# The low half of every weight block made by an adding DMA, in a two-layer decoder trunk on one core

## The chip, the cores and the metric

The kernel runs on one core of one Trainium2 chip. The metric is the device time of one execution in microseconds (us); lower is better. Before the change it is 1383.34 us, the median of three runs from 1379.25 to 1384.71 us.

The engines are named as in the profile: PE is TensorE's matrix multiply and PEld its weight load, DVE is VectorE, ACT is ScalarE, POOL is GpSimd, SP is SyncE. A "q" behind a name (SPq, POOLq) is that engine's sequencer, which waits and issues DMAs. L377 is line 377 of the kernel before. In the changed kernel the lines from 378 on are numbered one higher (L1191 of before is L1192 there), and the pair that is exchanged stands on L376 to L378.

## What is computed

The reference is a decoder trunk of two layers on a sequence of 512 tokens with a width of 1024, in float32. Cut to what matters:

```python
for l in range(2):
    hn = rms_norm(h, attn_norm[l])
    proj = hn @ w_in[l]                          # 1024 x 2592
    y_a = rwkv7_mixer(proj[..., :896], ...)      # delta-rule state, 4 heads of 64
    y_b = retention_mixer(proj[..., 896:1920], positions)
    y_c = mla_mixer(proj[..., 1920:], positions, ...)   # 8 heads, w_q_up and w_kv_up
    h = h + concat(y_a, y_b, y_c) @ w_out[l]     # 1024 x 1024
    gu = rms_norm(h, ffn_norm[l]) @ w_gate_up[l] # 1024 x 5632
    h = h + (silu(gu[..., :2816]) * gu[..., 2816:]) @ w_down[l]   # 2816 x 1024
return rms_norm(h, final_norm)
```

The large products are made with more than one pass of a reduced float32 format, "fp32r" in the profile. A factor x is written as a rounded part hi and a remainder lo, and a product w x is summed up from hi(w) hi(x), hi(w) lo(x) and lo(w) hi(x).

## The kernel before, in words

**Layout.** Activations are kept transposed, with features on the 128 partitions and the 512 tokens along a row. A product is a chain of 128 x 128 weight tiles, each multiplied into 128 x 512 activations, summed in a bank of PSUM.

**The weight stream.** All large weights lie in one long array in the order of use, cut into 204 blocks, most of them 128 partitions x 1024 floats (512 KB). For each block `load_next` (from L362) issues a DMA on SP into a raw tile `wr`, a rounding copy on ACT into `wh` (the hi part), and on DVE the subtraction `wr - wh` into `wl` (the lo part). For four blocks, 20, 30, 105 and 139, the subtraction is on POOL. Each of the three kinds of tile has three buffers. `wnext` (L380) keeps up to three converted blocks ready: whenever the program takes one, it queues the conversion of the next that is not yet ready. So the conversion of block n+2 is written down when block n is taken, and it must wait until PE has done with block n-1, whose buffers it takes over.

**The products.** `gemm` (L385) goes through the 128-row tiles of a block and issues three matmuls for each: `wh` with the high activations, `wh` with the low ones, `wl` with the high ones. PE runs in the order of the program, so `wl` is needed at the third matmul of a block. A full block is 24 matmuls. The blocks of the last part of the down projection have 768 columns and 18 matmuls.

**Stages.** In each layer come first the input projection with the three mixers (34 blocks), then the output projection, then the gate and up projections and the down projection, in three groups of 8, 8 and 6 blocks of 128 features. Two gate/up blocks make one block of hidden features: DVE scales both by the norm (L1188, L1190), ACT applies SiLU (L1189), POOL multiplies them (L1191), and `split` (L286 on ACT, L287 on DVE) makes their hi and lo parts. Before the gate and up projections POOL adds up squares for the norm (L316).

**What sets the order.** Each engine runs its own queue in order. The tile framework's scheduler places most instructions. Matmuls are pinned in program order. In the mixers several generators take turns in a small driver, with delays from the table `T`, and a table `EN` says which engine takes which small operation. The change touches neither table.

Of the kernel before, what the change touches and what calls it, by code (L numbers as in the profile page):

```python
# [11 lines left out]
F32 = mybir.dt.float32  # L12
# [3 lines left out]
AF = mybir.ActivationFunctionType  # L16
ALU = mybir.AluOpType
# [25 lines left out]
POOL_LO = (20, 30, 105, 139)  # L43
# [135 lines left out]
def tile_trunk(ctx: ExitStack, tc: tile.TileContext, a: dict, out: bass.AP, dbg=None):  # L179
    nc = tc.nc  # L180
    act, dve, pool, sp = nc.scalar, nc.vector, nc.gpsimd, nc.sync
# [20 lines left out]
    def nm(s):  # L202
        uid[0] += 1
        return f"{s}_{uid[0]}"
# [156 lines left out]
    def load_next(parts=1):  # L361
        if stream["next"] < len(shapes):  # L362
            i, j = shapes[stream["next"]]
            stream["next"] += 1
            t = wp.tile([P, i * j], F32, tag="wr", name=nm("wr"), bufs=NW)
            src = a["wts"][stream["off"] : stream["off"] + P * i * j].rearrange("(p n) -> p n", p=P)
            stream["off"] += P * i * j
            hi = wp.tile([P, i * j], F32R, tag="wh", name=nm("wh"))
            lo = wp.tile([P, i * j], F32R, tag="wl", name=nm("wl"))
            on = stream["next"] - 1  # L370
            for part in range(parts):
                z = slice(part * i * j // parts, (part + 1) * i * j // parts)
                stream["dma"] = sp.dma_start(t[:, z], src[:, z])
                if parts > 1:
                    tc.keep_in_program_order(stream["dma"])
                act.copy(hi[:, z], t[:, z])  # L376
                (pool if on in POOL_LO else dve).tensor_tensor(lo[:, z], t[:, z], hi[:, z].bitcast(F32), ALU.subtract)  # L377
            stream["ready"].append(tuple(z.rearrange("p (i j) -> p i j", i=i) for z in (hi, lo)))  # L378

    def wnext():  # L380
        while len(stream["ready"]) < 3 and stream["next"] < len(shapes):
            load_next()
        return stream["ready"].pop(0)
# [515 lines left out]
    def dense():  # L899
# [3 lines left out]
        for k in range(KT):  # L903
            if k < 2:
                tc.keep_in_program_order(sp.dma_start(h[0][:, k, :], a["xT"][:, k, :]))
                load_next(2) if k == 0 else None
            elif k % 2 == 0:
                tc.keep_in_program_order(sp.dma_start(h[k // 2], a["xT"][:, k : k + 2, :]))
                load_next(2) if k == 4 else None
            xg.append(pair(ua))  # L910
            act.activation(xg[k][0], hk(k), AF.Identity, scale=col("attn_norm", 0, k))
            dve.scalar_tensor_tensor(xg[k][1], hk(k), col("attn_norm", 0, k), xg[k][0].bitcast(F32), ALU.mult, ALU.subtract)
# [342 lines left out]
```

## Time and profile before

| | value |
|---|---|
| median of three runs | 1383.34 us (1379.25 to 1384.71) |
| the profiled execution's own time | 1382.67 us |
| its span, first to last instruction | 1380.9 us |
| mean granted TensorE clock | 0.982 |
| busy share of the span | PE 95%, DVE 58%, ACT 41%, POOL 17% |
| DMA | 130.84 MB, 95 GB/s on average |

The page of a profile lists busy time by engine, the span in 40 slices, the DMA queues, and the chain of work that ended last: beginning at the last instruction, each step goes back to what released it. A group's row reads: line, engine, operation, what it writes and reads, shape and count, then total busy time and the mean of one in ns, then the idle time of its engine just before, and what ended that. A row of the timeline starts with the start and the duration in us. A row of a view by windows gives the window, its length, and then for each engine the busy time with the number of instructions, the granted clock, the mean share of time that the 16 DMA engines were busy, and GB/s.

### The profile page before, as it was taken

The numbers are of one execution on the slowest core, as the hardware profiler recorded it, in microseconds if no ns is written. First come the engines' busy times: TensorE is split into PE (matmuls) and PEld (weight loads), VectorE is DVE, ScalarE is ACT, GpSimd is POOL, SyncE is SP. The second block draws the span as 40 slices with busy tenths as digits, with TensorE's granted clock in tenths as the row PEclk, the third lists the DMA queues.
The fourth block names the chain that finished last, engine by engine and source line by source line (L and its number), as shares of the span: only waits on it lengthen the run. The fifth ranks groups of instructions, "written<-read, shape, count | busy, mean of one in ns | idle before, by whom it ended". The sixth has DMA issues, their size and how long they took to land.

```text
span 1380.9 us, 16829 instructions
## 1 busy us (share of the span) xinstructions
PE 1313.5 (95%) x6478; PEld 1055.3 (76%) x6478; DVE 796.2 (58%) x1183; ACT 569.7 (41%) x944; POOL 238.7 (17%) x181
## 2 busy tenths in 40 slices
PE   7989988899999999999999898889999999999996
PEld 5778766578888888888877776756888888888884
DVE  7787856747544445344757696476564534543543
ACT  7844445826322232122575335367342212321333
POOL 1160321213110011001314401112131101100111
PEclk9999999999999999999999899999999999999998
DMA  6434421212222232322532424021233223333221
GB/s 235 125 99 140 96 76 32 77 61 92 97 102 92 92 107 92 101 97 73 174 97 81 111 85 85 31 85 54 76 107 105 94 92 95 104 93 105 89 80 61
DMA packets 65577, 130.84 MB, mean 95 GB/s; under 512 B 29044, under 2 KB 31764, under 8 KB 65496
## 3 DMA queue, kind: packets, MB, share of 16 engines
q1 hardware_dynamic: 64120, 128.14, 30.2%
q8 instruction: 51, 0.84, 0.3%
q10 hardware_dynamic: 1232, 1.09, 0.2%
q0 software_dynamic: 144, 0.52, 0.1%
q14 instruction: 30, 0.25, 0.1%
HBM read 117.40 MB, written 9.18 MB: 92 GB/s over the span
## 4 chain that ended last, share of the span: by engine, by line
PE 80%; DVE 10%; ACT 5%; issue 3%; POOL 1%; DMA 1%; SPq 0%; DVEq 0%; ACTq 0%; POOLq 0%
PE pd L232 72%; PE pm L232 7%; PE pm L239 1%; DVE wl L377 1%; DVE nmx L865 1%; DVE Sb L750 1%; ACT u L867 1%; ACT wh L376 1%; DVE u L608 1%; DMA wr<-in_wts_dram 0%; DVE r L296 0%; ACT L327 0%; ACT u L882 0%; DMA u<-in_xT_dram 0%; DVE u L609 0%
## 5 line engine op out<-in xcount | busy, mean ns | idle before, releaser
L232 PE MATMUL pd<-u,wh 128*128 128x512 f32 x3048 | 959.9, 396 | 7.6 <-ACT wh L376 6.4
L232 PEld LDWEIGHTS pd<-u,wh 128*128 128x128 f32 x3048 | 570.0, 189 | 135.3 <-issue 8.0
L232 PE MATMUL pd<-u,wl 128*128 128x512 f32 x1524 | 597.7, 392 | 0.0
L376 ACT CAST wh<-wr 128x1024 fp32r<-128x1024 f32 (+3 forms) x206 | 208.2, 1013 | 531.9 <-PE pd L232 353.9
L232 PEld LDWEIGHTS pd<-u,wl 128*128 128x128 f32 x1524 | 288.5, 189 | 61.0 <-DVE wl L377 0.2
L377 DVE TENSOR_TENSOR wl<-wr,wh 128x1024 fp32r<-128x1024 f32 (+3 forms) x202 | 283.3, 1404 | 59.8 <-ACT wh L376 57.0
L1191 POOL TENSOR_TENSOR r<-r,r 128x512 f32<-128x512 f32 x44 | 63.7, 1447 | 576.2 <-ACT wh L376 484.6
L1190 DVE TENSOR_TENSOR r<-pd,rB 128x512 f32<-128x512 f32 x44 | 30.4, 691 | 135.4 <-PE pd L232 135.4
L1197 DVE TENSOR_TENSOR u<-u,pd 128x512 f32<-128x512 f32 x48 | 33.0, 687 | 125.9 <-PE pd L232 125.9
L232 PE MATMUL pm<-u,u 32*32 32x32 f32 (+4 forms) x728 | 77.2, 287 | 24.9 <-DVE Sb L750 16.2
L232 PEld LDWEIGHTS pm<-u,u 32*32 32x32 f32 (+3 forms) x728 | 55.1, 162 | 48.6 <-DVE Sb L750 21.5
L316 POOL TENSOR_TENSOR acc<-acc,r 128x512 f32<-128x512 f32 x37 | 55.2, 1491 | 192.5 <-ACT r L315 192.1
L1188 DVE TENSOR_TENSOR r<-pd,rB 128x512 f32<-128x512 f32 x44 | 30.4, 691 | 67.7 <-PE pd L232 67.5
L286 ACT CAST u<-r 128x512 fp32r<-128x512 f32 x52 | 32.4, 623 | 78.5 <-POOL r L1191 63.5
L232 PE MATMUL pd<-u,u 96*128 96x512 f32 (+3 forms) x128 | 45.2, 459 | 2.7 <-ACT u L867 1.6
L287 DVE TENSOR_TENSOR u<-r,u 128x512 fp32r<-128x512 f32 x52 | 35.9, 689 | 18.9 <-ACT u L286 18.9
L239 PE MATMUL pm<-ident,u 128*128 128x128 f32 x188 | 33.5, 283 | 5.5 <-ACT r L773 2.0
L870 POOL TENSOR_SCALAR u<-u,rs 128x384 f32<-128x384 f32 x16 | 20.6, 1285 | 98.8 <-DVE rs L869 67.6
L865 DVE TENSOR_REDUCE nmx<-pd 128x1 f32<-128x256 f32 (+3 forms) x64 | 30.0, 481 | 11.7 <-PE pd L232 11.2
L239 PEld LDWEIGHTS pm<-ident,u 128*128 128x128 f32 x188 | 23.7, 145 | 13.1 <-ACT r L773 3.3
L321 DVE SCALAR_TENSOR_TENSOR u<-u,PC,u 128x512 fp32r<-128x512 f32 x24 | 32.0, 1342 | 2.6 <-ACT u L320 2.5
L867 ACT ACTIVATE u<-pd,nmx 128x512 f32<-128x512 f32 (+2 forms) x48 | 26.0, 546 | 11.9 <-DVE nmx L865 7.8
(243 smaller groups left out, 1142.9 us busy)
## 6 DMA issues: line engine op xcount, KB each, us to landing
wr<-in_wts_dram SPq DMA_DIRECT2D x174, 512.0 KB, 3.5
wr<-in_wts_dram SPq DMA_DIRECT2D x22, 384.0 KB, 3.1
u<-in_xT_dram SPq DMA_DIRECT2D x7, 512.0 KB, 6.7
tb<-tab_d SPq DMA_DIRECT2D x8, 256.0 KB, 4.9
r<-r SPq DMA_DIRECT2D x32, 64.0 KB, 2.0
h_d<-u SPq DMA_DIRECT2D x4, 512.0 KB, 2.6
u<-h_d SPq DMA_DIRECT2D x4, 512.0 KB, 3.6
wr<-in_wts_dram SPq DMA_DIRECT2D x4, 432.0 KB, 3.1
```

The costliest lines, as they stand in the source:

```text
L232: tc.keep_in_program_order(nc.tensor.matmul(o, lhsT, rhs, start=start, stop=stop, skip_group_check=True))
L239: tc.keep_in_program_order(nc.tensor.transpose(o, x, idn))
L286: act.copy(hi, src)
L287: E("e273").tensor_tensor(lo, src, hi.bitcast(F32), ALU.subtract)
L316: E("e302").tensor_tensor(acc, acc, q, ALU.add)
L321: dve.scalar_tensor_tensor(lo, t, g, hi.bitcast(F32), ALU.mult, ALU.subtract)
L376: act.copy(hi[:, z], t[:, z])
L377: (pool if on in POOL_LO else dve).tensor_tensor(lo[:, z], t[:, z], hi[:, z].bitcast(F32), ALU.subtract)
L865: dve.tensor_reduce(nmx, ps[:, 0:w], AX.X, ALU.max, negate=True)
L867: act.activation(pp[ib], ps[:, 0:w], AF.Exp, bias=nmx, accum_out=ssum)
L1191: E("e1171").tensor_tensor(t, t, u, ALU.mult)
L1197: dve.tensor_tensor(hk(m), hk(m), ps, ALU.add)
```

## The change

For every block, ACT now writes two tiles: first minus the raw weights into `wl` (an activation with scale -1, whose output is rounded to fp32r), then the rounded copy into `wh` as before. After the first of the two, a DMA issued on POOL's queue reads the same raw weights once more from HBM and adds them onto `wl`. The subtraction on DVE, or for four blocks on POOL, is gone, and the table `POOL_LO` is no longer used.

```diff
@@ -373,8 +373,9 @@
                 stream["dma"] = sp.dma_start(t[:, z], src[:, z])
                 if parts > 1:
                     tc.keep_in_program_order(stream["dma"])
+                act.activation(lo[:, z], t[:, z], AF.Identity, scale=-1.0)
+                pool.dma_start(lo[:, z], src[:, z], accum_op=ALU.add)
                 act.copy(hi[:, z], t[:, z])
-                (pool if on in POOL_LO else dve).tensor_tensor(lo[:, z], t[:, z], hi[:, z].bitcast(F32), ALU.subtract)
             stream["ready"].append(tuple(z.rearrange("p (i j) -> p i j", i=i) for z in (hi, lo)))
```

Two places show how the queues change. In these rows a number behind a tile's name only tells one buffer's use from another, and the brackets name the engines or DMA queues (DMAHW those of SP and ACT, DMASW that of POOL) whose semaphores the instruction waits for. The first place is POOL's queue at the first hidden features of layer 0. Before, it holds the sums of squares and the products alone:

```order
L316 TENSOR_TENSOR acc_2893<-acc_2893,r_661_3014 128x512 [waits Activation_49,Pool_49]
L1191 TENSOR_TENSOR r_679_3123<-r_679_3123,r_680_3124 128x512 [waits DVE_49,Activation_49]
L1191 TENSOR_TENSOR r_686_3163<-r_686_3163,r_687_3164 128x512 [waits DMAHW4_49,DVE_49,Activation_49]
L1191 TENSOR_TENSOR r_697_3234<-r_697_3234,r_698_3235 128x512 [waits DVE_49,Activation_49]
L1191 TENSOR_TENSOR r_708_3305<-r_708_3305,r_709_3306 128x512 [waits DVE_49,Activation_49]
```

The same place in the changed kernel:

```order
L316 TENSOR_TENSOR acc_2929<-acc_2929,r_658_3032 128x512 [waits Activation_49,Pool_49]
L316 TENSOR_TENSOR acc_2929<-acc_2929,r_661_3052 128x512 [waits Activation_49,Pool_49]
L377 DMA wl_3060<-in_wts_dram 128x1024 [waits DMASW4_49,Activation_49]
L377 DMA wl_3089<-in_wts_dram 128x1024 [waits DMASW5_49,Activation_49]
L377 DMA wl_3125<-in_wts_dram 128x1024 [waits DMASW6_49,Activation_49]
L377 DMA wl_3176<-in_wts_dram 128x1024 [waits DMASW7_49,Activation_49]
L1192 TENSOR_TENSOR r_679_3164<-r_679_3164,r_680_3165 128x512 [waits DVE_49,Activation_49]
L1192 TENSOR_TENSOR r_686_3205<-r_686_3205,r_687_3206 128x512 [waits DMAHW4_49,DVE_49,Activation_49]
L377 DMA wl_3217<-in_wts_dram 128x1024 [waits DMASW0_49,Activation_49]
L377 DMA wl_3249<-in_wts_dram 128x1024 [waits DMASW1_49,Activation_49]
L1192 TENSOR_TENSOR r_697_3278<-r_697_3278,r_698_3279 128x512 [waits DVE_49,Activation_49]
```

Between two products POOL now issues two adding DMAs. The first of each pair stands behind a product that waits for DVE and ACT.

The second place is ACT's queue at the start of the kernel, where the first two blocks are converted in halves. Before:

```order
L312 ACTIVATE acc_162<-u_72 128x512
L376 CAST wh_104<-wr_103 128x512 [waits DMAHW2_49]
L376 CAST wh_104<-wr_103 128x512 [waits DMAHW3_49]
L911 ACTIVATE u_116<-u_72,PC 128x512 [waits DMAHW4_49]
L911 ACTIVATE u_120<-u_73,PC 128x512 [waits DMAHW0_49]
```

In the changed kernel:

```order
L312 ACTIVATE acc_167<-u_72 128x512
L376 ACTIVATE wl_105<-wr_103 128x512 [waits DMAHW2_49]
L378 CAST wh_104<-wr_103 128x512
L376 ACTIVATE wl_105<-wr_103 128x512 [waits DMAHW3_49]
L378 CAST wh_104<-wr_103 128x512
L912 ACTIVATE u_118<-u_72,PC 128x512 [waits DMAHW4_49]
L912 ACTIVATE u_122<-u_73,PC 128x512 [waits DMAHW0_49]
```

Each half now passes through ACT twice, the negated copy first. The scaling of the inputs (L911, now L912) stands behind both.

## Prediction

> **What bounds the kernel now.** I read the page's busy times first, then a table by windows to separate the stages, then the chain of waits in the two mixers, then the timeline of single blocks.
>
> ```profile
> span 1380.9 us, 16829 instructions
> PE 1313.5 (95%) x6478; PEld 1055.3 (76%) x6478; DVE 796.2 (58%) x1183; ACT 569.7 (41%) x944; POOL 238.7 (17%) x181
> ```
>
> ```profile
> core 0: us, PE busy (x) PEld busy (x) DVE busy (x) ACT busy (x) POOL busy (x), PEclk, DMA share, GB/s
> 0.00:30.00 30.00, 23.09 (x77) 16.43 (x78) 22.45 (x34) 21.54 (x34) 6.67 (x12) 1.00 0.69 237
> 30.00:296.00 266.00, 242.60 (x1438) 190.56 (x1436) 194.09 (x384) 148.21 (x298) 62.22 (x48) 0.96 0.32 91
> 343.00:684.00 341.00, 340.64 (x1502) 281.45 (x1500) 162.42 (x162) 101.26 (x123) 39.93 (x27) 1.00 0.31 101
> 704.00:966.00 262.00, 238.89 (x1412) 183.48 (x1411) 183.44 (x370) 141.56 (x291) 60.69 (x48) 0.97 0.27 78
> 1016.00:1365.00 349.00, 348.64 (x1536) 287.72 (x1535) 158.39 (x155) 104.86 (x128) 40.76 (x29) 1.00 0.29 91
> ```
>
> In the two feed-forward stages (341 and 349 us) PE is idle for 0.4 us each: nothing done for DVE gains time there. In the two mixers (266 and 262 us) PE is idle 23 us each and DVE is busy for about 70% of the time, so a freed DVE can help there. The chain of waits inside these two windows says how much:
>
> ```profile
> by line: PE pd L232 42.5%; PE pm L232 16.6%; issue 4.4%; PE pm L239 4.0%; DVE wl L377 2.3%; DVE nmx L865 1.6%; DVE Sb L750 1.6%; ACT u L867 1.2%; DVE u L608 1.1%; POOL r L776 1.1%; DVE r L330 1.0%; DVE r L329 1.0%; DVE r L296 1.0%; DVE u L6
> by line: PE pd L232 31.5%; PE pm L232 17.6%; issue 7.5%; DVE nmx L865 3.3%; DVE wl L377 2.6%; PE pm L239 2.1%; ACT wh L376 1.8%; ACT u L867 1.8%; DVE u L608 1.6%; ACT L327 1.5%; DVE Sb L750 1.4%; DVE r L296 1.3%; ACT u L882 1.2%; DVE u L609
> ```
>
> The first row is the mixer of layer 0, the second that of layer 1. The subtraction L377 holds 2.3% of 266 us and 2.6% of 262 us of the chain: 6.1 + 6.8 = 12.9 us.
>
> **What the change moves.** Per full block these are the durations now:
>
> ```profile
> L376 ACT CAST wh<-wr 128x1024 fp32r<-128x1024 f32 x174 | 182.6, 1051 | 485.3 <-PE pd L232 327.9 <-issue 149.8 <-PE pm L232 7.2
> L377 DVE TENSOR_TENSOR wl<-wr,wh 128x1024 fp32r<-128x1024 f32 x170 | 253.6, 1492 | 57.7 <-ACT wh L376 55.1 <-DMA wr<-in_wts_dram 2.6
> L561 POOL DMA_DIRECT2D vf_d<-u x1: 749/749/749, 48.2 to 48.2; - x1
> vf_d<-u POOLq DMA_DIRECT2D x1, 512.0 KB, 4.0
> wr<-in_wts_dram SPq DMA_DIRECT2D x174, 512.0 KB, 3.5
> q1 hardware_dynamic: 64120, 128.14, 30.2%
> ```
>
> DVE loses its 1.49 us per block. ACT gains about another 1.05 us (the same shape as the cast). POOL gains 0.75 us of issuing, by the one DMA of 512 KB that it issues now, which lands 4.0 us after its issue. That DMA copies; an adding one stands nowhere in this trace. It must read the weights and the tile, then write. Queue q1's row gives the price of one pass: 30.2% of 1380.9 us for 128.14 MB, or 1.71 us for 0.524 MB on all 16 engines. So from issue to landing I bound it below by 4.0 us (adding is free) and above by 4.0 + 3 x 1.71 = 9.1 us (two more passes one behind the other, and a raw load in between). I take one more pass, 5.7 us, since the second read is the part that surely comes on top.
>
> [...]
>
> **Feed-forward: a longer latency under a long cover.** One steady block, and then a narrow one of the last down projection:
>
> ```profile
> 370.25 1.05 ACT L376 CAST wh<-wr 128x1024 fp32r<-128x1024 f32 x1 [3.86 <-issue]
> 371.27 1.28 POOL L1191 TENSOR_TENSOR r<-r,r 128x512 f32<-128x512 f32 x1 [9.60 <-DVE r L1190]
> 371.33 2.30 DVE L377 TENSOR_TENSOR wl<-wr,wh 128x1024 fp32r<-128x1024 f32 x1 [0.21 <-ACT wh L376]
> 375.69 1.05 ACT L376 CAST wh<-wr 128x1024 fp32r<-128x1024 f32 x1 [2.48 <-PE pd L232]
> 381.56 0.39 PE L232 MATMUL pd<-u,wl 128*128 128x512 f32 x1
> ```
>
> ```profile
> 1336.84 0.83 ACT L376 CAST wh<-wr 128x768 fp32r<-128x768 f32 x1 [1.36 <-PE pd L232]
> 1345.50 0.39 PE L232 MATMUL pd<-u,wl 128*128 128x512 f32 x1
> ```
>
> ACT converts the block at 370.25 as soon as PE has released its buffers, and PE first uses its low half at 381.56, two blocks of 5.44 us (370.25 to 375.69) and a little later. Now the low half is ready at 373.63. With the change ACT is done with it at 371.30, but POOL's order puts the product at 371.27 ahead of every second DMA, and it ends at 372.55. From there 381.56 leaves 9.0 us for a DMA of 5.7: 3.3 us to spare. The narrow block leaves 1345.50 - 1336.84 - 0.83 = 7.8 us for a DMA of three quarters of the bytes, 4.0 + 0.75 x 1.71 = 5.3. So in these stages I cost the edit at **0**. The cover is the two blocks ahead; without it, each us above 9.0 is paid every second block.
>
> The engines' room is thinner: per block one raw load of 1.71 us and two passes of 3.42 us make 5.13 of 5.44 us. The window 0 to 30 us moved 237 GB/s at a share of 0.69, or 1.53 us per pass, by which it is 4.6 of 5.44. Both fit, barely.
>
> **The start.**
>
> ```profile
> 5.74 0.60 ACT L376 CAST wh<-wr 128x512 fp32r<-128x512 f32 x1
> 7.41 0.63 PE L232 MATMUL pd<-u,wl 128*128 128x512 f32 x1
> 16.93 0.39 PE L232 MATMUL pd<-u,wl 128*128 128x512 f32 x1
> ```
>
> The first low half is wanted at 7.41, the second block's at 16.93. ACT ends the negated half at 5.74 + 0.60 = 6.34; with 5.7 us it lands at 12.0, 4.6 us late. The next matmuls then come faster than they did, because they waited for the input, but PE has stood still. I take **+4**, between 0 (the input's arrival hides it) and 8 (a landing in 9.1 us).
>
> **The places with little cover.** At the entry of the output and feed-forward stages the buffers come free late:
>
> ```profile
> 313.36 1.05 ACT L376 CAST wh<-wr 128x1024 fp32r<-128x1024 f32 x1 [8.51 <-PE pd L232]
> 320.60 0.39 PE L232 MATMUL pd<-u,wl 128*128 128x512 f32 x1
> 336.03 1.05 ACT L376 CAST wh<-wr 128x1024 fp32r<-128x1024 f32 x1 [4.26 <-issue]
> 343.49 0.39 PE L232 MATMUL pd<-u,wl 128*128 128x512 f32 x1
> ```
>
> Less the 1.05 us on ACT they leave 6.2 and 6.4 us for a DMA of 5.7, less what POOL does ahead of it (here the sums L316). Layer 1 has the same two stages. About 1 us each at four places is **+4**, between 0 and 4 x 2.9 = 12.
>
> **The mixers.** DVE gives back the chain's 12.9 us, less where PE itself waited for `wl` and now waits for a DMA: **-12**, between -5 and -18 (12.9 and the 4.7 us that ACT's cast, 1.8% of 262 us, holds ahead of it). ACT's second pass falls on the same queue as that cast, and hi comes 1.05 us later: another 4.7 us and something in layer 0, **+6**, between 0 and 12. The same two windows of L377 alone (DVE, then POOL) count the blocks:
>
> ```profile
> 30.00:296.00 266.00, 31.18 (x25) 4.90 (x2) 0.96 0.32 91
> 704.00:966.00 262.00, 29.25 (x24) 0.00 (x0) 0.97 0.27 78
> ```
>
> So POOL issues about 50 DMAs there, 50 x 0.75 = 38 us beside the 123 it is busy. Its queue is in order, so a DMA that waits for ACT, which waits for PE, holds up the mixer's products behind it. POOL's L776 is on the chain with 1.1% of 266 us, 2.9 us; I take **+4**, between 0 and 10.
>
> The sum is 4 + 4 - 12 + 6 + 4 = **+6 us**. The profiled execution took 1382.67 us, 0.67 below the median, so I forecast 1383.3 + 6, rounded to **1390 us**. All low ends together cannot be had; as the case's own range I take 1372 to 1406.
>
> **The rivals.**
>
> *The adding DMA lands late, not slowly* (17%). If it takes its upper 9.1 us, the start costs 8, each of the six tight places that I count in the timeline, the two quoted ones and four like them, 2.7 (9.1 + 1.05 - 7.46 at 336.03) or 16, the 14 narrow blocks after the first of each group about 0.4 or 5, every second of the 88 gate and up blocks (two to a hidden block) 0.1 or 4, and the mixers' terms stay near 0: about +35, 1420 us. For it speaks that each partition's row must be read before it is written; against it, that the copy on POOL's queue lands only 0.5 us after those of SP. It decides from about 7.8 us on. [...]
>
> *The DMA engines become the bound* (12%). With three passes for an adding DMA, a block needs 4 x 1.53 = 6.1 to 4 x 1.71 = 6.8 us of 5.44, and the 690 us of feed-forward stretch by 12 to 26%: +86 to +177, **1470 to 1560 us**. For it: 0.31 of the engines is already used there. Against it: writing and reading are counted once in a copy's pass. It decides from 3.7 us per adding DMA on.
>
> *The other side: the mixers gain all that DVE held* (16%). If a landing takes 5 us or less, the tight places cost nothing and the start 3. The chain passes from ACT's cast through L377 to the next DVE operation; both fall out of DVE's path, 12.9 + 4.7, and ACT and POOL, at 55% and 23% of these windows, absorb the rest: 3 - 18 = -15, **1368 us**. Against it: PE is busy for 91% of these windows anyway.
>
> **Chances.** A measurement of this kernel tells a difference from none above about 0.5%, 7 us. The forecast's case has 55%: 4 faster, 26 within, 25 slower by more than 7 us, as its range lies. Late landing 17 and bound engines 12 are slower; the other side is 14 faster and 2 within. Together 18% faster, 28% within, 54% slower. The range from 1368 to 1470 takes in the other side and the late landing, and leaves out the bound engines and a part of the other side.
>
> **What would show it.** The median landing of the `wl` rows among the DMA issues: below 7.8 us the feed-forward rows keep PE idle for less than 1 us. The engines' share in the feed-forward windows: about 0.85 with two passes, near 1 if they are the bound. PE's first use of `wl` at the start: near 12 us. In the mixers DVE's busy time falls by 60 us, ACT's rises by about 50, and L377 leaves the chain while POOL and ACT rows enter. The prediction is wrong if PE waits for `wl` in the steady feed-forward, or if the mixers shrink by more than 18 us.

## The result, and the profile after

The changed kernel takes **1433.88 us**, the median of four runs (1430.26 to 1437.78), against 1381.3 us for the kernel before beside it: 1.038 times as long, with a 95% interval of 1.0333 to 1.0427, or 53 us more. The forecast was 1390, slower, in a range from 1368 to 1470.

The page of the profiled execution begins as follows:

```profile
span 1436.0 us, 17393 instructions
...
PE 1332.6 (93%) x6478; PEld 1067.0 (74%) x6478; DVE 527.7 (37%) x981; ACT 754.1 (53%) x1150; POOL 388.7 (27%) x383
...
PE 70%; DMA 9%; issue 7%; DVE 6%; ACT 5%; POOL 1%; SPq 1%; DVEq 0%; POOLq 0%; ACTq 0%
```

The last row is the chain of waits by engine. Before, it was:

```profile
PE 80%; DVE 10%; ACT 5%; issue 3%; POOL 1%; DMA 1%; SPq 0%; DVEq 0%; ACTq 0%; POOLq 0%
```

DVE has lost a third of its work, and the kernel is slower. In the chain PE fell from 80 to 70%, DVE from 10 to 6%, and DMA rose from 1 to 9%. So the chain gave up DVE and took on DMA.

The DMA queues and issues tell what the adding costs (q0 is POOL's queue, q1 that of SP; the last number of an issue row is the median from issue to landing):

```profile
q0 software_dynamic: 29808, 103.82, 41.1%
q1 hardware_dynamic: 64120, 128.14, 31.2%
...
wr<-in_wts_dram SPq DMA_DIRECT2D x174, 512.0 KB, 5.3
wl<-in_wts_dram POOLq DMA_DIRECT2D x174, 512.0 KB, 7.6
...
xs_d<-r SPq DMA_DIRECT2D x8, 64.0 KB, 7.1
```

Before, that last row read:

```profile
xs_d<-r SPq DMA_DIRECT2D x8, 64.0 KB, 2.2
```

An adding DMA lands 7.6 us after its issue, not 5.7. Other transfers land later beside it: the raw load of a block takes 5.3 instead of 3.5 us, a row of 64 KB 7.1 instead of 2.2.

A table by windows shows where the time went. The windows are the stages of before, shifted to where they now lie (start, mixer, the entry of output projection and feed-forward, steady feed-forward; then the entry of layer 1, its mixer, its entry, its feed-forward):

```profile
0.00:49.00 49.00, 28.38 (x102) 21.08 (x103) 24.07 (x37) 33.11 (x50) 15.25 (x21) 0.93 0.82 230
49.00:316.00 267.00, 239.95 (x1412) 188.13 (x1410) 158.49 (x350) 163.02 (x314) 74.09 (x70) 0.95 0.58 132
316.00:379.00 63.00, 57.08 (x234) 44.80 (x234) 21.07 (x26) 33.64 (x43) 19.06 (x17) 0.92 0.70 158
379.00:714.00 335.00, 334.70 (x1475) 276.08 (x1473) 67.69 (x90) 153.69 (x180) 87.66 (x89) 1.00 0.87 193
...
745.00:1014.00 269.00, 240.51 (x1388) 183.54 (x1387) 156.69 (x339) 155.82 (x307) 76.94 (x71) 0.94 0.51 116
1014.00:1077.00 63.00, 59.09 (x251) 47.63 (x250) 23.05 (x29) 34.43 (x43) 19.15 (x18) 0.97 0.73 160
1077.00:1425.00 348.00, 345.67 (x1512) 284.21 (x1510) 60.09 (x87) 159.63 (x192) 89.56 (x91) 1.00 0.85 181
```

The two entries in the kernel before:

```profile
296.00:343.00 47.00, 47.00 (x211) 37.45 (x211) 28.13 (x29) 21.27 (x29) 11.22 (x7) 1.00 0.28 89
966.00:1016.00 50.00, 50.00 (x221) 41.18 (x221) 30.27 (x32) 19.00 (x26) 11.35 (x8) 1.00 0.27 85
```

In the steady feed-forward PE is as full as before, at a clock of 1.00, with the DMA engines at 0.87 and 0.85 (the 2.3 us that PE lacks in the last window lie behind the last block). Everything is lost elsewhere: 20.6 us of PE standing still in the first 49 us, 5.9 and 3.9 us in the entries, where it had stood still for none of the time, and a clock of 0.92 to 0.97 in the start, the entries and the mixers, where it had been 0.96 to 1.00.

PE's matmuls that read `wl` come in the order of the program, so each can be put down to its block. This table says how many us later PE is done with a block than in the kernel before, in the profiled executions:

```
after block           2     5    13    14    28    33    37   101   106   128   135   139   203
changed kernel     13.5  11.7  13.0  20.7  20.2  26.2  30.9  31.1  36.0  48.0  51.8  55.7  55.1
```

The loss comes in a few steps: 13.5 us by block 2, 7.7 at block 14, 6.0 and 4.9 at blocks 33 and 37, 12.0 over the second mixer (106 to 128), and so on; the 64 blocks from 38 to 101 add 0.2 together.

### The profile page after: what moved, and what is told of

Same layout as the page of the kernel before. It is cut to its first block, busy times and chain, and to the rows that moved or that the text cites. A ratio compares the mean times of both kernels' runs of the same rounds, so it can differ in the third digit from the quotient of the medians.

```text
span 1436.0 us, 17393 instructions
## 1 busy us (share of the span) xinstructions
PE 1332.6 (93%) x6478; PEld 1067.0 (74%) x6478; DVE 527.7 (37%) x981; ACT 754.1 (53%) x1150; POOL 388.7 (27%) x383
## 3 DMA queue, kind: packets, MB, share of 16 engines
q0 software_dynamic: 29808, 103.82, 41.1%
## 4 chain that ended last, share of the span: by engine, by line
PE 70%; DMA 9%; issue 7%; DVE 6%; ACT 5%; POOL 1%; SPq 1%; DVEq 0%; POOLq 0%; ACTq 0%
PE pd L232 63%; PE pm L232 5%; DMA wl<-in_wts_dram 4%; DMA r<-in_exact_dram 1%; PE pm L239 1%; DMA r<-r 1%; DMA xs_d<-r 1%; ACT wl L376 1%; DMA u<-xs_d 1%; DVE nmx L866 1%; DMA r<-in_rw_g_dram 1%; SPq L988 1%; DVE Sb L751 1%; POOL acc L316 0%; ACT wh L378 0%
## 5 line engine op out<-in xcount | busy, mean ns | idle before, releaser
L377 POOL DMA_DIRECT2D wl<-in_wts_dram x206 | 179.5, 872 | 641.2 <-ACT wl L376 625.3
L376 ACT ACTIVATE wl<-wr 128x1024 fp32r<-128x1024 f32 (+3 forms) x206 | 208.9, 1015 | 7.9 <-PE pd L232 6.1
L232 PE MATMUL pm<-u,u 32*32 32x32 f32 (+4 forms) x728 | 79.5, 293 | 31.6 <-DVE Sb L751 16.1
L1192 POOL TENSOR_TENSOR r<-r,r 128x512 f32<-128x512 f32 x44 | 56.8, 1291 | 151.0 <-ACT wh L378 113.5
L232 PE MATMUL pd<-u,u 96*128 96x512 f32 (+3 forms) x128 | 48.5, 488 | 3.8 <-DVE u L1131 2.2
L329 DVE SCALAR_TENSOR_TENSOR r<-r,r 128x512 f32<-128x512 f32 x20 | 14.8, 741 | 58.6 <-ACT r L328 55.9
```

The lines of the kernel that those rows point to most:

```text
L232: tc.keep_in_program_order(nc.tensor.matmul(o, lhsT, rhs, start=start, stop=stop, skip_group_check=True))
L376: act.activation(lo[:, z], t[:, z], AF.Identity, scale=-1.0)
L377: pool.dma_start(lo[:, z], src[:, z], accum_op=ALU.add)
L1192: E("e1171").tensor_tensor(t, t, u, ALU.mult)
```

## The experiments

Three theories stood against each other. **Cover:** the low half lands later than the two blocks ahead can hide, at a few places. **POOL's queue:** sums and products stand behind a DMA that waits for ACT, which waits for PE. **Traffic:** the DMA engines are full. All times are medians; each ratio is against the kernel before on the same chip (1382.6 to 1383.0 us).

### The adding DMA in one stage at a time

Four kernels use the adding DMA for some blocks only and subtract the others as before. The edit of the kernel before is the same in each, with another set of numbers in `DMA_LO`:

```diff
-                act.copy(hi[:, z], t[:, z])
-                (pool if on in POOL_LO else dve).tensor_tensor(lo[:, z], t[:, z], hi[:, z].bitcast(F32), ALU.subtract)
+                if on in DMA_LO:
+                    act.activation(lo[:, z], t[:, z], AF.Identity, scale=-1.0)
+                    pool.dma_start(lo[:, z], src[:, z], accum_op=ALU.add)
+                    act.copy(hi[:, z], t[:, z])
+                else:
+                    act.copy(hi[:, z], t[:, z])
+                    (pool if on in POOL_LO else dve).tensor_tensor(lo[:, z], t[:, z], hi[:, z].bitcast(F32), ALU.subtract)
```

> The adding DMA makes the low half of blocks 0 to 4 alone; all other blocks are subtracted on DVE or POOL as before. By blocks, the changed kernel's PE is 18 us behind the kernel before at its ninth block, so if the start is a loss of its own: +14 to +18 us over before. If the start's delay is hidden again by waits of the mixer that follows: within 5 us of before.

> The adding DMA for blocks 5 to 28 and 107 to 130 alone, the two mixers. Theory (POOL's in-order queue and the late landing hurt where chains are short of cover): +12 to +22 us. Rival (DVE's relief outweighs, the loss lies elsewhere): -15 to 0 us.

> The adding DMA for blocks 29 to 38, 102 to 106 and 131 to 140 alone: the output projections, the first blocks of each feed-forward and of layer 1. Theory (too little cover for a landing of 7.6 us): +14 to +24 us, with PE waiting for the low halves. Rival (these delays come from work that arrives late out of the mixers): within 5 us of before.

> The adding DMA for blocks 39 to 101 and 141 to 203 alone, the steady feed-forward: 126 of the 204 blocks. Theory (two blocks of cover hide a landing of 7.6 us): within 3 us of before, perhaps 2 us faster in the narrow blocks. Rival (late landing or the traffic costs here too): +10 us or more.

| adding DMA in | blocks | us | ratio, 95% interval | over before |
|---|---|---|---|---|
| the start | 5 | 1396.18 | 1.0094 (1.0065 to 1.0123) | +13.2 |
| the mixers | 48 | 1400.26 | 1.0140 (1.0111 to 1.0169) | +17.3 |
| the entries | 25 | 1404.16 | 1.0157 (1.0135 to 1.0179) | +21.2 |
| the steady feed-forward | 126 | 1382.45 | 1.0001 (0.9986 to 1.0017) | -0.5 |

The four add up to 51.2 us, about what the whole change cost. The start came out 0.8 us under what was expected, the others inside. The 126 blocks of the feed-forward are free. Its DMA share is the same as in the changed kernel, which takes the traffic theory out of this stage:

```profile
345.00:686.00 341.00, 341.00 (x1501) 280.98 (x1500) 73.62 (x96) 157.25 (x185) 90.36 (x91) 1.00 0.87 195
```

The 25 blocks of the entries cost most, and the timeline of this kernel shows how. In it lines are numbered higher (L233 is PE's matmul, L317 the sum of squares). Here block 33 is late:

```profile
319.59 0.79 PE L233 MATMUL pd<-u,wl 128*128 128x512 f32 x1 [2.67 <-DMA wl<-in_wts_dram]
320.18 1.05 PE L233 MATMUL pd<-u,wh 128*128 128x512 f32 x2
321.04 0.63 PE L233 MATMUL pd<-u,wl 128*128 128x512 f32 x1
...
324.88 0.63 PE L233 MATMUL pd<-u,wl 128*128 128x512 f32 x1
...
326.69 0.39 PE L233 MATMUL pd<-u,wl 128*128 128x512 f32 x1
```

PE waits 2.67 us for the DMA. This is how that DMA came to be issued, on ACT and then on POOL:

```profile
309.53 1.05 ACT L380 CAST wh<-wr 128x1024 fp32r<-128x1024 f32 x1 [7.51 <-issue]
310.48 1.05 ACT L378 ACTIVATE wl<-wr 128x1024 fp32r<-128x1024 f32 x1
...
311.83 0.85 POOL L379 DMA_DIRECT2D wl<-in_wts_dram  x1 [8.68 <-ACT wl L378]
```

The low half lands at 319.55, 7.72 us after its issue. The program writes the negated copy first, but the framework's scheduler has placed the cast ahead of it here, which costs the low half 0.95 us. That is the rule and not the exception: in the changed kernel's trace the cast comes first in 172 of 206 conversions, and at six of the seven late blocks of the entries (33, 37, 102, 105, 135 and 139, not 136). A kernel with the order of the two pinned was not run.

After the wait PE's matmuls take 0.63 us instead of 0.39 for more than five us. By windows, the granted clock in that stretch is half:

```profile
320.00:325.30 5.30, 5.30 (x13) 4.05 (x13) 1.69 (x3) 2.61 (x4) 2.52 (x3) 0.50 0.96 207
325.70:331.00 5.30, 5.30 (x24) 4.36 (x23) 2.54 (x3) 2.99 (x5) 2.58 (x2) 0.99 0.46 123
```

In 5.30 us PE had 13 matmuls in work at the clock of 0.50 and 24 at 0.99. So a wait of 2.7 us becomes a step of 5.8.

### Is it the clock?

In the kernel of the entries, PE now makes 60 matmuls more, into a bank of PSUM that nobody reads, where it had stood still:

```diff
             mm(ps, wh, xl, False, False)
+            for _ in range(warm_of(w) if first and i == 0 else 0):
+                tc.keep_in_program_order(nc.tensor.matmul(spare[0], wh, xh, start=True, stop=True, skip_group_check=True))
             mm(ps, wl, xh, False, last and i == n - 1)
```

(`warm_of` gives the number for the block at hand; the lines that count the blocks are left out.)

> The kernel with the adding DMA in blocks 29 to 38, 102 to 106 and 131 to 140 alone (1404.2 us), in which PE now makes 60 matmuls more, into a spare bank that nobody reads, just before it first wants the low halves of blocks 33, 37, 105, 135 and 139: 12, 16, 17, 7 and 8 of them, about as long as PE stood still there. Theory (a pause of 2 to 4 us makes the granted clock fall to 0.50 for 3.4 or 6.8 us after it, which doubles the price of the wait): 1391 to 1397 us, though PE does more. Rival (the slow matmuls after a pause have another cause, such as the landing itself): 1402 to 1408 us.

It took 1401.57 us, 1.0137 (1.0101 to 1.0172): outside what either theory expected, and not to be told from 1404.16. At blocks 33, 37 and 105 the theory held. The granted clock in two windows over blocks 33 and 37 is 1.00:

```profile
322.00:328.00 6.00, 5.77 (x26) 4.43 (x25) 5.93 (x5) 5.29 (x8) 5.63 (x5) 1.00 0.73 158
346.00:352.00 6.00, 6.00 (x28) 4.97 (x27) 3.85 (x6) 4.84 (x6) 0.00 (x0) 1.00 0.93 186
```

The steps there:

```
step at block                33    37   102   105  135+136   139   sum
entries alone               5.8   5.6   1.2   5.7     3.7    3.8  25.8
with matmuls in the wait    3.3   3.6   4.8   4.3     4.1    3.1  23.2
```

At 33, 37 and 105 PE does more work and loses 5.9 us less. The low halves come no earlier for it: the first matmul with block 33's starts 3.1 us after the end of block 32 in the entries' kernel and 3.4 us after it here, and the rest of the block then takes 8.2 and 5.3 us. At 135 to 139 the added matmuls change little (0.4 more and 0.7 less). At block 102, where none were added, a landing came later this time and took 3.6 back, with a clock of 0.50 behind a wait of 2.9 us.

The places without added matmuls make a second test. In the changed kernel and in that of the entries PE waits 13 times for the first low half of a late block. All five waits of 2.7 us and more, and three of the four of 1.9 to 2.1 us, are followed by a granted clock of 0.50, and the steps there are 1.5 to 2.2 times the wait. After the four of 1.7 us or less the clock stays at 1.00, and it does after the fourth of 2.1 us, at block 105 of the changed kernel, whose step is 2.4 us.

So the halved clock is shown as the second part of a step; how much it costs over the whole kernel, these runs cannot tell. The granted clock's mean fell from 0.982 to 0.966 in the profiled executions and to 0.966 to 0.977 in the four of the changed kernel, which makes 8 to 24 us of lost clock more than before, some of it while PE stood still.

### More cover

The first attempt put the low halves' matmuls behind all others of a product, which gives a full block 14 matmuls, 3.2 us, more cover. Its control does the same to the kernel before.

```diff
-            wl = lo[:, kw, :] if wsl is None else wsl(lo, kw)
             mm(ps, wh, xh, first and i == 0, False)
             mm(ps, wh, xl, False, False)
-            mm(ps, wl, xh, False, last and i == n - 1)
+            yield 0
+        for i, (kw, kx) in enumerate(ks):
+            wl = lo[:, kw, :] if wsl is None else wsl(lo, kw)
+            mm(ps, wl, x[kx][0], False, last and i == n - 1)
             yield 0
```

> The changed kernel, with each product's matmuls in another order: first all that use the high half of a block, then all that use its low half. A full block then wants its low half at the 17th matmul instead of the third, 14 x 0.227 = 3.2 us later. Theory (PE waits 2 to 4 us for low halves that land 7.6 us after their issue, at few places): most of the waits at the output projections and feed-forward entries go, some in the mixers: 1400 to 1415 us against 1434 for the changed kernel. Rival (POOL's queue and the traffic are the loss, not the cover): 1425 us or more.

> The kernel before with the same order of matmuls, low halves last. It is the control for the run before it: if the order itself is worth nothing where low halves are early, within 5 us of before; all that the order gains on the changed kernel is then cover.

They took 1461.35 us, 1.0572 (1.0540 to 1.0604), and the control 1451.44 us, 1.0495 (1.0468 to 1.0522). Both expectations failed. The edit does a second thing besides, it gives the driver twice as many turns, and the control falls 41 us behind by block 28, in the first mixer, and 17 more between blocks 101 and 134, over the second. Whether it is the turns or the order that the mixers don't bear was not tried. The two kernels differ by 10 us where the change had cost 53, but with losses of that size on top the difference is no measure of the cover.

So the next kernel puts them last only for blocks 30 to 101 and 132 to 203 (for these `later` is true), with no more turns than before:

```diff
             mm(ps, wh, xl, False, False)
-            mm(ps, wl, xh, False, last and i == n - 1)
+            if not later:
+                mm(ps, wl, xh, False, last and i == n - 1)
             yield 0
+        for i, (kw, kx) in enumerate(ks if later else ()):
+            mm(ps, lo[:, kw, :], x[kx][0], False, last and i == n - 1)
```

> The changed kernel with the low halves' matmuls last in each product, but only for the blocks of the output projections and the feed-forward (30 to 101 and 132 to 203), with no more turns of the driver than before, so that the mixers keep their order. Theory (3.2 us more cover is what these places lack): the 10.7 and 7.7 us that PE falls behind there in the changed kernel go, 1412 to 1420 us. Rival (something else holds PE there): 1428 us or more.

It took 1423.37 us, 1.0301 (1.0279 to 1.0324), 10.5 us less than the changed kernel and 3 above the range. PE's loss at the two entries shrank as expected:

```
step over blocks           28 to 38   134 to 140
changed kernel                 10.7          7.7
low halves last there           1.5          1.0
```

So cover is what these places lack: 3.2 us more of it takes 16 of 18 us away. The kernel as a whole gains less, 10.5 us in the medians. The two profiled executions do differ by 16.1 us (1419.9 against 1436.0), but 3.6 of these lie in the start and the first mixer, where nothing was changed, and 3.4 us of what the entries gain are lost again in the steady feed-forward.

### POOL's queue

The changed kernel with all operations that the table gives to POOL moved to DVE (the table has 15, not 16 as the text below says):

```diff
-EN = {'e499': 'd', ... 'e542': 'p', 'e563': 'p', 'e564': 'p', ... 'e1171': 'p', 'e302': 'p', ...}
+EN = {'e499': 'd', ... 'e542': 'd', 'e563': 'd', 'e564': 'd', ... 'e1171': 'd', 'e302': 'd', ...}
```

> The changed kernel with all 16 small operations that the table EN gives to POOL moved to DVE, which the change has freed: POOL keeps the adding DMAs and little else, so hardly any sum or product waits behind a DMA that waits for ACT. Theory (POOL's in-order queue makes the larger part of the loss at the start and in the mixers): 1408 to 1422 us. Rival (the landing time and the engines' traffic make it): 1429 to 1440 us.

1417.25 us, 1.0246 (1.0211 to 1.0281): 16.6 us less than the changed kernel, within the theory's range. The start shows the mechanism. These are the timeline's rows of POOL in the changed kernel (start, length, and in brackets the time stood still before and what ended it):

```profile
31.06 0.89 POOL L377 DMA_DIRECT2D wl<-in_wts_dram  x1 [9.30 <-ACT wl L376]
31.73 1.53 POOL L316 TENSOR_TENSOR acc<-acc,r 128x512 f32<-128x512 f32 x1
32.94 1.16 POOL L377 DMA_DIRECT2D wl<-in_wts_dram  x1
33.70 1.70 POOL L316 TENSOR_TENSOR acc<-acc,r 128x512 f32<-128x512 f32 x1
```

And PE's in the same stretch:

```profile
35.45 2.08 PE L232 MATMUL pm<-acc,C 128*128 128x512 f32 x2 [6.39 <-POOL acc L316]
```

POOL stands still for 9.30 us before the DMA of block 3, which waits for ACT. The last two sums of squares stand behind it, and PE then waits 6.39 us for them. ACT's rows say why it came late:

```profile
24.20 0.62 ACT L919 CAST EX<-r 128x512 fp32r<-128x512 f32 x1 [4.24 <-DMA r<-in_exact_dram]
...
28.77 1.03 ACT L378 CAST wh<-wr 128x1024 fp32r<-128x1024 f32 x1
29.71 1.05 ACT L376 ACTIVATE wl<-wr 128x1024 fp32r<-128x1024 f32 x1
```

ACT had stood 4.24 us for an input, `r<-in_exact_dram`, issued at 8.72 and awaited until 24.18; it then works through its queue without a pause up to block 3's two copies, the cast first. In the kernel before, the same cast ran at 17.49 without a wait. In the two kernels without the addition that come below it ran at 18.25 (no DMA) and 19.22 (a copying one), so it is the adding that holds this input up; the engines' share is 0.82 in the first 49 us. PE had ended block 0, whose buffers block 3 takes over, at 28.37, only 0.4 us before ACT came to them. So at the start several delays end together: PE's first blocks, late by a wait of 7.25 us for the first low half, the input on which ACT stood, and POOL's order.

With the sums on DVE the step by block 2 is 5.6 instead of 13.5 us. But little of that lasts: PE then waits 3.25 us for a later low half, and after block 13 this kernel is 11.2 us behind, the changed one 13.0. The gain lies in the mixers, above all at block 14:

```profile
119.44 1.05 ACT L376 ACTIVATE wl<-wr 128x1024 fp32r<-128x1024 f32 x1
...
122.22 1.30 POOL L990 TENSOR_TENSOR r<-r,tb 128x512 f32<-128x512 f32 x1 [3.41 <-DMA r<-r]
123.48 0.84 POOL L377 DMA_DIRECT2D wl<-in_wts_dram  x1
...
132.07 0.79 PE L232 MATMUL pd<-u,wl 128*128 128x512 f32 x1 [5.09 <-DMA wl<-in_wts_dram]
```

The adding DMA could go at 120.49, when ACT is done, but stands behind a product that waits for a transfer, and goes 3.0 us later, of the 5.09 that PE waits for it. With the product on DVE this step is 1.2 instead of 7.7 us. At the entries the edit helps little: blocks 33, 37 and 105 cost 3.3, 4.5 and 4.9 us here, and 6.0, 4.9 and 2.4 in the changed kernel. There it is cover.

One rival stays open. The same edit makes each operation faster: a sum of squares takes 0.69 us on DVE and 1.48 on POOL. How much of the 16.6 us is this and how much the queue was not parted, as the kernel before was not run with this table.

```profile
L316 POOL TENSOR_TENSOR acc<-acc,r 128x512 f32<-128x512 f32 x37 | 54.8, 1481 | 43.3 <-ACT r L315 42.7
L316 DVE TENSOR_TENSOR acc<-acc,r 128x512 f32<-128x512 f32 x37 | 25.5, 688 | 18.4 <-ACT r L315 18.0
```

(The first row is the changed kernel's, the second this one's.)

### What the adding itself costs

One kernel leaves the DMA out, so that ScalarE's minus rounded weights stay as they are; another lets POOL's DMA copy the weights over the low half instead of adding them.

```diff
-                pool.dma_start(lo[:, z], src[:, z], accum_op=ALU.add)
```

> The changed kernel without its DMA: ACT still writes minus the rounded weights and the rounded weights, nothing is added, so the low halves are wrong and what is left out is the addition. It has the change's gain (DVE is free of the subtraction) and one of its costs (ACT's second pass) alone. By the prediction's terms, -12 and +6: 1372 to 1384 us. Rival (ACT's second pass costs the mixers more than DVE gives back): 1390 us or more.

```diff
-                pool.dma_start(lo[:, z], src[:, z], accum_op=ALU.add)
+                pool.dma_start(lo[:, z], src[:, z])
```

> The changed kernel with POOL's DMA copying the weights over the low half instead of adding them: the same issue, the same wait for ACT and the same write, without the second read; the low halves are then the weights themselves, and what is left out is the addition. Theory (the adding is what makes 4.0 us into 7.6): it lands in 4.5 to 6.0 us and the kernel takes 1395 to 1415 us. Rival (it is POOL's path and the raw loads beside it): 7 us and 1428 us or more.

Without the DMA: 1386.78 us, 1.0021 (1.0003 to 1.0038). With the copy: 1394.89 us, 1.0081 (1.0066 to 1.0097), 0.1 us below its range. The copy's queue and issues:

```profile
q0 software_dynamic: 29808, 103.82, 22.1%
...
wr<-in_wts_dram SPq DMA_DIRECT2D x174, 512.0 KB, 3.6
wl<-in_wts_dram POOLq DMA_DIRECT2D x174, 512.0 KB, 4.6
```

And POOL's issuing of them, in the view by groups (busy time and mean ns of one, then the idle time before them and what ended it):

```profile
L377 POOL DMA_DIRECT2D wl<-in_wts_dram x206 | 114.6, 556 | 665.2 <-ACT wl L376 647.4 <-ACT LR L286 6.9 <-ACT u L754 6.3
```

The same bytes by the same queue land in 4.6 us when they are copied and in 7.6 us when they are added. In engine time, 22.1% of 1393.8 us is 308 us for the copies and 41.1% of 1436.0 is 590 us for the adding ones: 1.92 times as much.

So the 53 us are put together of about 4 for a second pass on ACT, less all that DVE gave back, 8 for a DMA on POOL's queue, and 39 for the adding, with all that hangs on it: the later landing, the engines' longer work, POOL's longer issue. Of what the copying kernel loses, 8.6 us stand after block 13 already. The 4 are a sum of two signs: without the DMA the first mixer gains 2.8 us (blocks 2 to 28) and the second loses 6.1 (106 to 128). The expectation for the kernel without the DMA failed: it held that the change's gain alone would be a gain or nothing (1372 to 1384), and it is a loss of 0.2%, small and clear of 0.

### All mendings together

> The changed kernel with three mendings: the low halves last as in the run before it, POOL's small operations on DVE, and the first five blocks subtracted on DVE. If the losses found so far add up (16.6 for POOL's queue, 18 for the cover, 9 left at the start): 1386 to 1396 us, about level with the kernel before. If they overlap: 1400 us or more. Faster than before (under 1376 us) only if the freed DVE is worth over 10 us in the mixers.

The edits are those of the low halves last, of POOL's operations on DVE, and `if on > 4` around the adding DMA. 1399.95 us, 1.0121 (1.0103 to 1.0139): 34 us of the 53 come back and the kernel before is still the faster one. It lies between the two ranges, at the edge of the upper one. The single gains that the expectation adds up include 18 us for the cover; with the 10.5 that it gave in the medians they come to 1398, so no overlap is shown by the total. One is seen at block 14: its step, which POOL's queue being free had made 1.2, is 6.7 here, in another order of the mixer. The kernel without any DMA is no faster than the one before, so in this order of the mixers a landing hidden entirely would not make the change pay. Whether another division of the work over the freed DVE would was not tried.

## Why the prediction was right or wrong

**Right: nothing is lost in the steady feed-forward.** The prediction costed it at 0, with a landing of up to 9.0 us covered. The landing was 7.6 and the stage alone measured 1.0001. The engines' share was forecast at about 0.85 for two passes and is 0.87 and 0.85. The rival of bound engines needed 3.7 us per adding DMA; 590 us for 103.82 MB are 2.98 us for 0.524 MB.

**Mis-sized: the landing.** The term was 4.0 for the copy plus 1.71 for a second read, 5.7. Measured are 4.6 and 3.0, 7.6. No row shows the second read itself; what the runs show is the engine time of 1.92 copies. Bounds of 4.0 and 9.1 held it. The rival "lands late" had put the point from which it decides at 7.8, and its sum at 1420: nearest to what came, and given 17%. That point was taken from the narrow blocks; the entries, with 6.2 and 6.4 us of cover, are passed already at 7.6. That its sum came so near is in part luck: it had about 9 us for the feed-forward, which lost nothing, and none for the mixers, which lost 17. (Of the 9, the 0.4 us for each narrow block do not come out of its own terms: 4.0 + 0.75 x 5.13 is 7.85 us, against a cover of 7.8.) The landing is no later in the mixers than elsewhere: its median for 512 KB is 7.5 and 7.0 us in their two windows and 7.6 in the steady feed-forward.

**Mis-sized: the places with little cover.** +4 us at four places of 1 us each; measured alone, +21.2 at about six. By the prediction's own arithmetic a landing of 7.6 gives 1.4 us at block 33; PE waited for 2.7 there and lost 5.8. Most of the 1.3 us between is the cast, which the working had behind the negated copy and which ran ahead of it. The other 3.1 are the halved clock after the wait, which the working left out altogether.

**Mis-sized: the start.** +4, at most 8; measured alone, +13.2. The late first low half was seen (12.0 forecast, 15.45 in the changed kernel), with 8.7 us for a landing among the input's loads. Two things were not seen: that another input, `r<-in_exact_dram`, lands late beside the adding DMAs and holds ACT for 4.24 us (though PE frees the buffers hardly earlier), and that the sums of squares stand on POOL's queue behind a DMA that waits for ACT. The prediction named the second mechanism for the mixers and did not look for it at the start, although the order of POOL's instructions shows it there. As only 1.8 us of the start's loss are gone after block 13 with the sums on DVE, the landing and the traffic make most of it; these two were not parted.

**Failed: the mixers.** -12 for DVE, +6 for ACT and +4 for POOL made -2; measured alone, they cost +17.3. DVE's busy time in the two windows did fall as forecast, from 378 to 315 us (ACT's rose by 29 and not by 50). But the kernel without the DMA shows that the freed DVE and ACT's second pass together are worth +4 and not -6. The step that failed is the price read off the chain: the 12.9 us of L377 on it were counted as time to be gained, and 4.7 us as what ACT's pass adds there. Whether less than 12 us came back or the pass cost more than 6 stays open, as no run has one without the other. What the DMA itself then costs the mixers shows in the chain of the first one in the changed kernel:

```profile
by line: PE pd L232 32.5%; PE pm L232 14.3%; issue 6.0%; DMA r<-r 4.1%; PE pm L239 4.0%; DMA wl<-in_wts_dram 3.2%; DMA u<-xs_d 3.0%; DMA xs_d<-r 2.8%; DMA r<-in_rw_g_dram 2.0%; ACT wl L376 1.9%; SPq L988 1.9%; DVE Sb L751 1.7%; DVE nmx L866
```

The low halves hold 3.2% of it, and transfers of the mixer's own, `r<-r`, `u<-xs_d`, `xs_d<-r` and `r<-in_rw_g_dram`, 11.9%; none of these stands in the row of before that the prediction shows. Block 14's 7.7 us add POOL's queue to a late landing. How much of the mixers' loss is traffic was not separated.

**Right: the sign, and the range, but not the sum.** The forecast was +6 us and the result +53. The likeliest case (55%) was too small by 44 us and its own range, 1372 to 1406, did not hold; the range to 1470 did because it was drawn to take in the late landing. That the other side, faster by what DVE gave up, had little chance was right for a reason that was given, PE being busy for 91% of the mixers.

## What to carry to other kernels

The conversion that moved here from DVE to a DMA traded 1.49 us of work for a landing 7.6 us after the issue. For such a move go through the places where the buffers come free late, not through the steady loop: here 126 of 204 blocks hid 7.6 us for nothing, and 25 others paid 21 us. Before costing a freed engine as a gain, leave the new transfer out and measure what is left; here the freed DVE and ACT's added pass together gave a loss of 4 us. Price a wait on PE with the clock behind it: at block 33 a wait of 2.67 us became a step of 5.8. Look for what stands behind a DMA on a queue that also computes: at the start POOL stood 9.30 us before the DMA of block 3, with two sums of squares behind it for which PE waited 6.39 us. And look in the trace whether the scheduler kept the order that the cover was worked out with: here it did not in 172 of 206 conversions.

## What the runs showed of the hardware

**Behind most of PE's longer waits at the entries the granted clock was 0.50.** Eight of nine waits of 1.9 to 3.8 us there were followed by a granted clock of 0.50 for 3.4 or 6.8 us, in which matmuls started every 0.43 instead of 0.227 us, and the steps came to 1.5 to 2.2 times the wait. None of four waits of 0.8 to 1.7 us was followed by it. Nor was the wait of 3.25 us at the start of the kernel with the sums on DVE: behind it matmuls started every 0.23 us.

**The adding DMAs took 1.92 times the engine time of the copying ones**, 590 us against 308, and landed 3.0 us later for 512 KB, 7.6 us after the issue. POOL was busy 872 ns with an issue instead of 556:

```profile
L377 POOL DMA_DIRECT2D wl<-in_wts_dram x206 | 179.5, 872 | 641.2 <-ACT wl L376 625.3
```

**At a share of 0.87 the DMA engines still kept up** with a block every 5.44 us in the steady feed-forward, though the raw loads took 5.3 instead of 3.5 us (medians of the whole kernel).
